# A raised scheduler priority for the ScalarE and VectorE steps of an RWKV-7 state passage

## The chip, the cores and the metric

The kernel runs on one core of a Trainium2 chip. The metric is the device time of one execution in microseconds (us). Engines are called PE (TensorE, matmuls), PEld (TensorE's weight loads), DVE (VectorE), ACT (ScalarE), POOL (GpSimd) and SP (SyncE, which here only issues transfers).

## The reference, cut to what matters

One layer of a hybrid trunk over 2048 tokens of width 1024. A token mixer takes one combined projection of the normed input and has three branches: chunked attention (4 heads), forgetting attention (4 heads) and RWKV-7 time mixing (8 heads). An output projection and a gated feed-forward part follow. The change touches the RWKV-7 branch alone, whose core is a recurrence over time:

```
def rwkv7_step(S, inp):
    r, w, k, v, kk, kka = inp
    sa = jnp.einsum('bhvk,bhk->bhv', S, -kk)
    S = S * w[:, :, None, :] + sa[..., None] * kka[:, :, None, :] + v[..., None] * k[:, :, None, :]
    y = jnp.einsum('bhvk,bhk->bhv', S, r)
    return S, y
...
    _, y = lax.scan(rwkv7_step, S0, xs)
```

## The kernel before

The program has three stages after one another: the input projection with the RWKV-7 branch (here called the mixer stage), then attention, then the output projection and the feed-forward part. Only the mixer stage is of interest.

The mixer stage handles 4 blocks of 512 tokens, and in each block 4 pairs of heads, so 16 rounds. A round of the recurrence is split into chunks of 64 tokens, 8 to a block. Three generators make the instructions of a round:

- `rwkv_front` projects the inputs (the matmuls of lines 281 to 283 in `project`), and forms decays, keys and the products of chunk with chunk (lines 411 to 507, most of them on DVE).
- `rwkv_inverse` inverts the triangular matrices of the chunks, by 31 pairs of small DVE operations that depend on one another (lines 533 and 536), and then by transfers and a few matmuls.
- `rwkv_back` carries the state through. It copies right-hand sides (`R`, line 608 by the helper of line 157), multiplies by the inverse (line 611), evicts `W` (line 157) and `UV` (line 616), multiplies again (line 626), forms `QA` (lines 634 and 637) and then goes through the 8 chunks: matmuls into `z` (lines 652 and 653), then the state `S` is rewritten by one ACT step (line 655) and one DVE step (line 656), and the next chunk's matmuls read it. The 16 rounds have 128 of these steps. After every 4 chunks the outputs are evicted into `Y` (line 658 on ACT, line 157 on DVE). All `z` of 4 chunks lie in one PSUM bank (`ZB = 1`).

The function `weave` writes these generators' instructions into one program: a back part and an inverse part of the round before go in between the projection matmuls of the present round. A back part that has issued a step yields a number of projection matmuls (`NEED`; 6 after each state step) before its next instructions are written.

This written order is not the order on the engines. A planner gives each instruction a number, in the order in which it is written. It then plays the program through by its own durations and, for each engine, takes the instruction with the lowest number among those whose inputs are there. What comes out is one fixed queue for each engine, which the chip then runs in that order, whatever the real durations are. Where an instruction's input is late on the chip, the whole queue of its engine waits.

Of the kernel before, what the change touches and what calls it, by code (L numbers as in the profile page):

```python
# [14 lines left out]
AF = mybir.ActivationFunctionType  # L15
ALU = mybir.AluOpType
# [4 lines left out]
P = 128  # L21
# [7 lines left out]
LEV = {'acc': G_, 'w': G_, 'kka': V, 'kf': V, 'rk': V, 'n': V, 'l': V, 'ql': V, 'ak': G_, 'gn': V, 'kr': V, 'uv': S_, 'r': V, 'w_': V, 'y': V, 'dt': V, 'bp': V, 'qa': V}  # L29
# [67 lines left out]
def trunk_kernel(ctx: ExitStack, tc: tile.TileContext, xT, w_in, pp, cst, cau, rel, relr, w2, a2, g2, w_out, w_up, w_down, out, dbg=None):  # L97
    nc = tc.nc
# [14 lines left out]
    def par(name, i=0):  # L113
        a = PP[name][0] + i
        return pps[:, a : a + 1]

    def cn(name):
        a, b = CC[name]
        return csts[:, a:b] if b <= 256 else cst1[:, a - 256 : b - 256]
# [36 lines left out]
    def copy(e, out, in_):  # L156
        e.copy(out, in_) if e is nc.scalar else e.tensor_copy(out=out, in_=in_)
# [79 lines left out]
    for r in range(NR):  # L237
        KR = c1.tile([P, 2, 8, 64], F32, name=f"KR{r}")
# [12 lines left out]
    for i in range(4):  # L251
        S = c1.tile([P, P], F32, name=f"S{i}")
# [259 lines left out]
    def rwkv_inverse(s):  # L512
# [53 lines left out]
        for c, e in ((0, nc.scalar), (1, LEV['dt'](nc))):  # L566
            rows = slice(c * 64, c * 64 + 32)
            copy(e, DT[rows, :, c * 64 + 32 : c * 64 + 64], ps[rows].rearrange("p w s i -> p (w s) i"))

    def rwkv_back(s):  # L570

        b, i, lg, KR, DT, LZ, v, bD, EC = (s[n] for n in ("b", "i", "lg", "KR", "DT", "LZ", "v", "bD", "EC"))
        S = Ss[i]
        Yt = t512("Y", "bp")
        Y = Yt.rearrange("p (a h d) -> p a h d", a=4, h=2)
        halves = (0, 2)
        UVs, Rs, Ws, QAs = {}, {}, {}, {}

        for p0 in halves:
            ps = psm["b"].tile([P, 2, 2, 2, 64], F32, name="rw", tag="ps")  # L580
            for a_ in range(2):
                pr = p0 + a_
                nc.tensor.transpose(ps[:, 0, a_].rearrange("p h d -> p (h d)"), v[:, pr * P : (pr + 1) * P], ident)
                nc.tensor.transpose(ps[:, 1, a_].rearrange("p h d -> p (h d)"), KR[:, 0, pr * 2 : pr * 2 + 2, :].rearrange("p c t -> p (c t)"), ident)
            UV = UVs[p0] = t512("UV", "bk").rearrange("p (a h c d) -> p a h c d", a=2, h=2, c=2)
            nc.scalar.copy(UV[64:128, :, :, 0, :], ps[0:64, 0])
            copy(LEV['uv'](nc), UV[0:64, :, :, 1, :], ps[64:128, 0])
            R = Rs[p0] = t512("R", "bk")
            nc.scalar.copy(R.rearrange("p (u s d) -> p u s d", u=4, s=2)[:, :, 0, :], ps[:, 1].rearrange("p a h d -> p (a h) d"))
        yield NEED[0]  # L590

        for p0 in halves:
            ps = psm["b"].tile([P, 4, 64], F32, name="rw", tag="ps")
            for u in range(4):
                a_, hp = divmod(u, 2)
                for c in range(2):
                    o = 64 - c * 64
                    mm(
                        ps[c * 64 : c * 64 + 64, u, :],
                        LZ[o : o + 64, p0 + a_, hp, c, 0, :],  # L600
                        UVs[p0][o : o + 64, a_, hp, c, :],
                        start=True,
                        stop=True,
                    )
            copy(LEV['r'](nc), Rs[p0].rearrange("p (u s d) -> p u s d", u=4, s=2)[:, :, 1, :], ps)
        yield NEED[1]
        yield NEED[3]
        for p0 in halves:
            ps = psm["b"].tile([P, 4, 2, 64], F32, name="rw", tag="ps")
            for u in range(4):  # L610
                mm(ps[:, u].rearrange("p s d -> p (s d)"), DT[:, p0 * 2 + u, :], Rs[p0][:, u * P : (u + 1) * P], start=True, stop=True)
            W = Ws[p0] = qd.tile([P, 4, 64], F32, name="W", tag="W")
            copy(LEV['w_'](nc), W, ps[:, :, 0, :])
            for c in range(2):
                rows = slice(c * 64, c * 64 + 64)
                nc.scalar.mul(UVs[p0][rows, :, :, c, :].rearrange("p a h d -> p (a h) d"), ps[rows, :, 1, :], -1.0)
        yield NEED[4]

        for p0 in halves:
            QA = QAs[p0] = t512("QA", "bk").rearrange("p (a c n) -> p a c n", a=2, c=2)  # L620
            pcs = [psm["b"].tile([P, 2, P], F32, name="rw", tag="ps") for c in range(2)]
            for u in range(4):
                a_, hp = divmod(u, 2)
                for c, ps in enumerate(pcs):
                    rows = slice(c * 64, c * 64 + 64)
                    mm(
                        ps[hp * 64 : hp * 64 + 64, a_, :],
                        Ws[p0][rows, u, :],
                        LZ[rows, p0 + a_, hp, c, 1:3, :],
                        start=True,  # L630
                        stop=True,
                    )
            for c, ps in enumerate(pcs):
                nc.vector.tensor_tensor(
                    QA[:, :, c, 0:64], KR[:, 1, p0 * 2 + c : p0 * 2 + 4 : 2, :], ps[:, :, 0:64], op=ALU.subtract
                )
                nc.vector.tensor_tensor(
                    QA[:, :, c, 64:128], cn("ident2").unsqueeze(1).to_broadcast([P, 2, 64]), ps[:, :, 64:128], op=ALU.subtract
                )
        yield NEED[5]  # L640

        for p0 in halves:
            if ZB == 2:
                zz = [ps_z.tile([P, 2, 2, 64], F32, name="z", tag="z") for c in range(2)]
            else:
                zt = ps_z.tile([P, 2, 2, 2, 64], F32, name="z", tag="z")
                zz = [zt[:, :, c] for c in range(2)]
            steps = [(a_, c) for a_ in range(2) for c in range(2)]
            for a_, c in steps:
                zs = zz[c][:, a_].rearrange("p h d -> p (h d)")  # L650
                for hp in range(2):
                    mm(zz[c][:, a_, hp, :], LZ[:, p0 + a_, hp, c, 1:3, :], UVs[p0][:, a_, hp, c, :], start=(hp == 0), stop=False)  # L652
                mm(zs, QAs[p0][:, a_, c, :], S, start=False, stop=True)
                ch = (p0 + a_) * 2 + c
                nc.scalar.activation(S[0:64, 0:64], zs[64:128, 0:64], AF.Identity, scale=EC[64:128, 0, ch : ch + 1])
                nc.vector.tensor_scalar(S[64:128, 64:128], zs[64:128, 64:128], EC[64:128, 1, ch : ch + 1], None, op0=ALU.mult)
                yield NEED[6]
            nc.scalar.copy(Y[0:64, p0 : p0 + 2], zz[0][0:64])
            copy(LEV['y'](nc), Y[64:128, p0 : p0 + 2], zz[1][0:64])

        Y8 = Y.rearrange("p a h d -> p (a h) d")
        st = sp.tile([P, 8], F32, name="st")
        nc.vector.tensor_reduce(st, Y8, axis=AX.X, op=ALU.add)
        nc.vector.tensor_scalar(st, st, 1.0 / 64, None, op0=ALU.mult)
        nc.vector.tensor_tensor(Y8, Y8, st.unsqueeze(2).to_broadcast([P, 8, 64]), op=ALU.subtract)
        ysq = t512("ysq", "bp")
        nc.scalar.activation(ysq, Yt, AF.Square)
        st2 = sp.tile([P, 8], F32, name="st2")
        nc.vector.tensor_reduce(st2, ysq.rearrange("p (g d) -> p g d", d=64), axis=AX.X, op=ALU.add)
        nc.scalar.activation(st2, st2, AF.Ln, scale=1.0 / 64, bias=eps[:, 1:2])  # L670
        nc.scalar.activation(st2, st2, AF.Exp, scale=-0.5)
        LEV['gn'](nc).tensor_tensor(Y8, Y8, st2.unsqueeze(2).to_broadcast([P, 8, 64]), op=ALU.mult)
        yield NEED[7]
        ps = psm["b"].tile([P, TB], F32, name="rw", tag="ps")
        for pr in range(4):
            nc.tensor.transpose(ps[:, pr * P : (pr + 1) * P], Y[:, pr].rearrange("p h d -> p (h d)"), ident)
        yl = t512("yl", "bp")
        nc.scalar.activation(yl, ps, AF.Identity, scale=par("lnx_g", i), bias=par("lnx_b", i))
        bv = t512("bv", "bp")
        nc.sync.dma_start(out=bv, in_=bD)  # L680
        nc.gpsimd.tensor_tensor(yl, yl, bv, op=ALU.add)
        gps = psm["b"].tile([P, TB], F32, name="rw", tag="ps")
        mm(gps, gg[:, i * P : (i + 1) * P], lg, start=True, stop=True)
        nc.vector.tensor_tensor(yl, yl, gps, op=ALU.mult)
        nc.gpsimd.dma_start(out=yD[512 + i * P : 512 + (i + 1) * P, b * TB : (b + 1) * TB], in_=yl)
# [505 lines left out]
    work, todo, Y = iter(()), None, None  # L1191
# [280 lines left out]
```

## Time and profile before

| | us |
|---|---|
| median of 3 runs (lowest, highest) | 3211.55 (3209.77, 3211.91) |
| the profiled execution, its own time | 3213.01 |
| its span, from the first to the last instruction | 3211.2 |
| the mixer stage, of the span | 0 to about 1175 |
| PE busy, of the span | 3017.4 (94%) |
| DVE busy, of the span | 2368.5 (74%) |
| ACT busy, of the span | 1394.9 (43%) |

The profile is one execution. In its rows a time of start is in us from the span's start. In a timeline a bracket behind a row gives the idle time of that engine just before it and the instruction whose end closed it. In the view of waits a row reads: who waited, for whom, us in total, how many times, and the longest.

### The profile page before, as it was taken

The page shows a single profiled execution, that of the slowest core. Times are in us where ns is not written, and L with a number is a line of the kernel's source. Part 1 is how long each engine was busy: PE and PEld are TensorE (multiplying, and loading weights), DVE is VectorE, ACT ScalarE, POOL GpSimd, SP SyncE. Part 2 cuts the span into 40 slices and gives each one's busy share as a digit, 9 for nine tenths or more (in the row PEclk, how much of TensorE's full clock was granted, in tenths as well). Part 3 has the DMA queues.
Part 4 walks back from the last instruction along what each step waited for, and adds up shares of the span by engine and source line. Part 5 has one row for each costly group of instructions (what it writes and reads, how often), then busy time and mean ns, then how long its engine had stood idle before and what let it go on. Part 6 is the DMA issues. An engine that isn't in the chain of part 4 may idle for free.

```text
span 3211.2 us, 49128 instructions
## 1 busy us (share of the span) xinstructions
PE 3017.4 (94%) x17820; PEld 2638.9 (82%) x17820; DVE 2368.5 (74%) x4590; ACT 1394.9 (43%) x2610; POOL 950.1 (30%) x928
## 2 busy tenths in 40 slices
PE   6988989998999979999989999999999998999999
PEld 4766767776767756677789899998899998999998
DVE  6667666756676646777553788889988889988886
ACT  5434444544444335578532343334333334333332
POOL 1010010001001021144242444444444444444443
PEclk8988999999999989999999999999999999999999
DMA  7756755656644576523234322222422222422221
GB/s 223 213 154 179 207 165 150 175 151 177 171 120 125 143 177 152 139 73 86 73 103 151 132 79 80 79 69 77 158 79 80 79 79 81 136 73 79 79 80 68
DMA packets 310818, 392.92 MB, mean 122 GB/s; under 512 B 137144, under 2 KB 228804, under 8 KB 299752
## 3 DMA queue, kind: packets, MB, share of 16 engines
q1 hardware_dynamic: 305936, 378.44, 40.0%
q0 software_dynamic: 2816, 8.39, 0.9%
q10 hardware_dynamic: 1824, 2.95, 0.4%
q8 instruction: 141, 2.31, 0.3%
q14 instruction: 101, 0.83, 0.1%
HBM read 304.65 MB, written 86.36 MB: 122 GB/s over the span
## 4 chain that ended last, share of the span: by engine, by line
PE 67%; DVE 17%; issue 5%; ACT 4%; DMA 4%; POOL 2%; SPq 1%; POOLq 0%; DVEq 0%; ACTq 0%
PE ps L1299 7%; PE ps L1298 7%; PE ps L1297 7%; PE ps L1345 4%; PE ps L1343 4%; PE ps L1344 4%; PE mm L282 2%; PE mm L281 2%; PE mm L283 2%; PE o L1069 2%; DVE tm L533 2%; DVE T L536 2%; PE z L652 2%; PE ps L1205 2%; PE ps L1206 2%
## 5 line engine op out<-in xcount | busy, mean ns | idle before, releaser
L1299 PE MATMUL ps<-B,wu 128*128 128x340 f32 (+1 forms) x1848 | 594.0, 321 | 19.6 <-DVE wu L161 19.4
L1297 PE MATMUL ps<-B,wu 128*128 128x340 f32 (+1 forms) x1848 | 589.7, 319 | 1.9 <-ACT wu L160 1.8
L1298 PE MATMUL ps<-B,wu 128*128 128x340 f32 (+1 forms) x1848 | 590.5, 320 | 0.0
L1299 PEld LDWEIGHTS ps<-B,wu 128*128 128x128 f32 x1848 | 348.7, 189 | 27.9 <-DVE wu L161 27.5
L1343 PE MATMUL ps<-hid,wd 128*128 128x340 f32 (+1 forms) x1056 | 341.9, 324 | 13.4 <-ACT wd L160 10.2
L1297 PEld LDWEIGHTS ps<-B,wu 128*128 128x128 f32 x1848 | 348.7, 189 | 2.6 <-ACT wu L160 2.1
L1298 PEld LDWEIGHTS ps<-B,wu 128*128 128x128 f32 x1848 | 347.8, 188 | 0.1
L1345 PE MATMUL ps<-hid,wd 128*128 128x340 f32 (+1 forms) x1056 | 338.8, 322 | 3.8 <-POOL wd L161 3.7
L1344 PE MATMUL ps<-hid,wd 128*128 128x340 f32 (+1 forms) x1056 | 340.1, 322 | 0.0
L281 PE MATMUL mm<-hT,w 128*128 128x512 f32 x704 | 314.5, 447 | 22.4 <-ACT w L160 16.0
L161 DVE TENSOR_TENSOR wu<-S,wu 128x512 fp32r<-128x512 f32 x264 | 258.0, 984 | 74.3 <-ACT wu L160 74.3
L282 PE MATMUL mm<-hT,w 128*128 128x512 f32 x704 | 291.2, 414 | 7.8 <-DVE hT L161 6.6
L283 PE MATMUL mm<-hT,w 128*128 128x512 f32 x704 | 291.3, 414 | 1.2 <-DVE w L161 1.1
L1346 DVE TENSOR_TENSOR acc<-acc,ps 128x340 f32<-128x340 f32 (+1 forms) x528 | 247.1, 502 | 48.1 <-PE ps L1345 47.8
L161 POOL TENSOR_TENSOR wd<-raw,wd 128x1024 fp32r<-128x1024 f32 x66 | 171.3, 2618 | 269.4 <-ACT wd L160 267.8
L160 ACT CAST wu<-S 128x512 fp32r<-128x512 f32 x264 | 162.9, 618 | 151.2 <-PE ps L1299 140.7
L1343 PEld LDWEIGHTS ps<-hid,wd 128*128 128x128 f32 x1056 | 201.6, 191 | 16.4 <-ACT wd L160 11.1
L1345 PEld LDWEIGHTS ps<-hid,wd 128*128 128x128 f32 x1056 | 201.6, 191 | 6.1 <-POOL wd L161 6.1
L161 DVE TENSOR_TENSOR wu<-raw,wu 128x512 fp32r<-128x512 f32 x198 | 201.1, 1017 | 5.6 <-ACT wu L160 5.6
L1344 PEld LDWEIGHTS ps<-hid,wd 128*128 128x128 f32 x1056 | 201.8, 191 | 0.0
L281 PEld LDWEIGHTS mm<-hT,w 128*128 128x128 f32 x704 | 138.8, 197 | 66.9 <-ACT w L160 17.0
L160 ACT CAST wu<-raw 128x512 fp32r<-128x512 f32 x198 | 120.7, 620 | 162.0 <-PE ps L1299 142.1
(337 smaller groups left out, 6814.2 us busy)
## 6 DMA issues: line engine op xcount, KB each, us to landing
w<-wD SPq DMA_DIRECT2D x72, 1024.0 KB, 6.6
raw<-in_w_up_dram SPq DMA_DIRECT2D x132, 512.0 KB, 3.6
raw<-in_w_down_dram SPq DMA_DIRECT2D x66, 512.0 KB, 3.6
wD<-w SPq DMA_DIRECT2D x24, 1024.0 KB, 5.5
wraw<-in_w_in_dram SPq DMA_DIRECT2D x24, 512.0 KB, 6.3
xt<-in_xT_dram SPq DMA_DIRECT2D x48, 256.0 KB, 4.2
K<-qkD SPq DMA_DIRECT2D x21, 512.0 KB, 8.3
Q<-qkD SPq DMA_DIRECT2D x84, 128.0 KB, 2.9
```

The costliest lines, as they stand in the source:

```text
L160: (hi_eng or nc.scalar).copy(hi, src) if (hi_eng or nc.scalar) is nc.scalar else hi_eng.tensor_copy(out=hi, in_=src)
L161: (lo_eng or nc.vector).tensor_tensor(lo, src, f(hi), op=ALU.subtract)
L281: mm(ps, hi[:, kt, 0:P], hT[kt][:, 0, :], start=(kt == 0), stop=False)
L282: mm(ps, hi[:, kt, 0:P], hT[kt][:, 1, :], start=False, stop=False)
L283: mm(ps, lo[:, kt, 0:P], hT[kt][:, 0, :], start=False, stop=(kt == KT - 1))
L1297: mm(ps, whl[:, 0, kt, :], Bs[p][:, kt, 0, 0:n], start=(kt == 0), stop=False)
L1298: mm(ps, whl[:, 0, kt, :], Bs[p][:, kt, 1, 0:n], start=False, stop=False)
L1299: mm(ps, whl[:, 1, kt, :], Bs[p][:, kt, 0, 0:n], start=False, stop=(kt == 3))
L1343: mm(ps, wd[:, 0, ch], hid[:, 0, cs], start=(u == 0), stop=False)
L1344: mm(ps, wd[:, 0, ch], hid[:, 1, cs], start=False, stop=False)
L1345: mm(ps, wd[:, 1, ch], hid[:, 0, cs], start=False, stop=(u == G - 1))
L1346: nc.vector.tensor_tensor(acc[ct][:, cs], acc[ct][:, cs], ps, op=ALU.add)
```

## The change

A context manager lowers the planner's number of every instruction written inside it by 200 and restores it on exit. It is put around the evictions and state steps of `rwkv_back`: `R` (one half of it), `W`, `UV`, `QA`, `S` on both engines, and `Y` on both engines. Matmuls, transfers and all other generators keep their numbers. No instruction is added, removed or altered; no tile is allocated inside the blocks.

```diff
+    def urgent():
+        return tc.high_priority(offset=200)
+
     def rwkv_back(s):
...
-            copy(LEV['r'](nc), Rs[p0].rearrange("p (u s d) -> p u s d", u=4, s=2)[:, :, 1, :], ps)
+            with urgent():
+                copy(LEV['r'](nc), Rs[p0].rearrange("p (u s d) -> p u s d", u=4, s=2)[:, :, 1, :], ps)
...
-            copy(LEV['w_'](nc), W, ps[:, :, 0, :])
-            for c in range(2):
-                rows = slice(c * 64, c * 64 + 64)
-                nc.scalar.mul(UVs[p0][rows, :, :, c, :].rearrange("p a h d -> p (a h) d"), ps[rows, :, 1, :], -1.0)
+            with urgent():
+                copy(LEV['w_'](nc), W, ps[:, :, 0, :])
+                for c in range(2):
+                    rows = slice(c * 64, c * 64 + 64)
+                    nc.scalar.mul(UVs[p0][rows, :, :, c, :].rearrange("p a h d -> p (a h) d"), ps[rows, :, 1, :], -1.0)
...
             for c, ps in enumerate(pcs):
-                nc.vector.tensor_tensor(
-                    QA[:, :, c, 0:64], KR[:, 1, p0 * 2 + c : p0 * 2 + 4 : 2, :], ps[:, :, 0:64], op=ALU.subtract
-                )
...
+                with urgent():
+                    nc.vector.tensor_tensor(
+                        QA[:, :, c, 0:64], KR[:, 1, p0 * 2 + c : p0 * 2 + 4 : 2, :], ps[:, :, 0:64], op=ALU.subtract
+                    )
...
                 ch = (p0 + a_) * 2 + c
-                nc.scalar.activation(S[0:64, 0:64], zs[64:128, 0:64], AF.Identity, scale=EC[64:128, 0, ch : ch + 1])
-                nc.vector.tensor_scalar(S[64:128, 64:128], zs[64:128, 64:128], EC[64:128, 1, ch : ch + 1], None, op0=ALU.mult)
+                with urgent():
+                    nc.scalar.activation(S[0:64, 0:64], zs[64:128, 0:64], AF.Identity, scale=EC[64:128, 0, ch : ch + 1])
+                    nc.vector.tensor_scalar(S[64:128, 64:128], zs[64:128, 64:128], EC[64:128, 1, ch : ch + 1], None, op0=ALU.mult)
                 yield NEED[6]
-            nc.scalar.copy(Y[0:64, p0 : p0 + 2], zz[0][0:64])
-            copy(LEV['y'](nc), Y[64:128, p0 : p0 + 2], zz[1][0:64])
+            with urgent():
+                nc.scalar.copy(Y[0:64, p0 : p0 + 2], zz[0][0:64])
+                copy(LEV['y'](nc), Y[64:128, p0 : p0 + 2], zz[1][0:64])
```

## Rows read from the trace of the kernel before

**Rows 1.** Mixer stage: us, busy (count) of PE PEld DVE ACT POOL, PEclk, DMA.

```profile
0.00:1175.00 1175.00, 1063.04 (x6266) 823.88 (x6266) 770.23 (x2173) 521.63 (x1073) 112.06 (x189) 0.94 0.60 167
```

**Rows 2.** The chain of work that ended last, from 1160 to 1212.

```profile
1173.90 0.86 PE rw L683 x2
...
1190.93 13.45 DMA TR<-exttD
```

**Rows 3.** Waits of PE in the mixer stage, 0 to 1175.

```profile
PE z L652 <- DVE S L656: 22.2, 18, 5.8
...
PE mm L282 <- DVE hT L161: 6.6, 3, 3.8
PE z L652 <- DVE Y L157: 6.0, 7, 2.0
...
PE z L652 <- ACT UV L616: 3.3, 3, 1.9
...
PE rw L683 <- DVE DT L157: 0.6, 1, 0.6
```

**Rows 4.** ACT's idle before line 655; line 656's durations, DVE's idle before it.

```profile
  PE z L653: 153.5, 97
...
L656 DVE TENSOR_SCALAR S<-z,EC x128: 290/291/294, 160.4 to 1165.4; 64x64 f32<-64x64 f32 x128
...
  ACT S L655: 58.3, 56
```

**Rows 5.** Timelines around the longest wait: PE and ACT, 455 to 478.

```profile
459.04 1.02 PE L427 MATMUL mm<-sq,cst 128*128 128x512 f32 x2
...
460.97 0.44 PE L653 MATMUL z<-S,QA 128*128 128x128 f32 x2
...
461.17 0.48 PE L281 MATMUL mm<-hT,w 128*128 128x512 f32 x1
...
467.28 0.39 PE L283 MATMUL mm<-hT,w 128*128 128x512 f32 x1
473.47 1.08 PE L652 MATMUL z<-UV,LZ 128*128 128x64 f32 x4 [5.80 <-DVE S L656]
...
463.23 0.31 ACT L655 ACTIVATE S<-z,EC 64x64 f32<-64x64 f32 x1
```

**Rows 6.** Timeline of DVE in that stretch: first and last before the step.

```profile
463.37 0.21 DVE L297 SCALAR_TENSOR_TENSOR r<-carry,pps,r 128x1 f32<-128x1 f32 x1
...
471.76 1.25 DVE L533 TENSOR_TENSOR tm<-T,NT 128x35 f32<-128x35 f32 x1
473.04 0.29 DVE L656 TENSOR_SCALAR S<-z,EC 64x64 f32<-64x64 f32 x1
```

**Rows 7.** Busy time and clock in and behind that wait (columns: Rows 1).

```profile
465.00:472.20 7.20, 2.67 (x12) 1.85 (x10) 7.20 (x12) 1.95 (x3) 5.01 (x5) 1.00 0.77 265
472.20:479.00 6.80, 5.53 (x20) 4.52 (x20) 4.22 (x15) 0.62 (x2) 0.75 (x1) 0.50 0.03 10
```

**Rows 8.** Timeline, 738 to 752: the two next waits, and what DVE ran.

```profile
743.36 0.66 PE L652 MATMUL z<-UV,LZ 128*128 128x64 f32 x4 [2.52 <-DVE S L656]
...
744.33 0.31 ACT L655 ACTIVATE S<-z,EC 64x64 f32<-64x64 f32 x1 [0.86 <-PE z L653]
...
749.76 0.29 DVE L656 TENSOR_SCALAR S<-z,EC 64x64 f32<-64x64 f32 x1
...
750.11 0.66 PE L652 MATMUL z<-UV,LZ 128*128 128x64 f32 x4 [3.01 <-DVE S L656]
```

**Rows 9.** Timeline, 408 to 412: a wait behind an operation that already runs.

```profile
409.11 1.56 DVE L438 TENSOR_SCALAR a<-a,pps,oka 128x512 f32<-128x512 f32 x1
...
411.05 0.66 PE L652 MATMUL z<-UV,LZ 128*128 128x64 f32 x4 [0.41 <-DVE S L656]
```

**Rows 10.** Timelines of PE: a wait with nothing in the way, one behind ACT.

```profile
309.03 1.12 PE L652 MATMUL z<-UV,LZ 128*128 128x64 f32 x4 [0.73 <-DVE S L656]
...
522.94 0.43 PE L652 MATMUL z<-UV,LZ 128*128 128x64 f32 x2 [1.90 <-ACT UV L616]
```

More of the change, by code (lines that the diff above doesn't have):

```diff
@@ L633, in rwkv_back @@
             for c, ps in enumerate(pcs):
-                nc.vector.tensor_tensor(
-                    QA[:, :, c, 0:64], KR[:, 1, p0 * 2 + c : p0 * 2 + 4 : 2, :], ps[:, :, 0:64], op=ALU.subtract
-                )
-                nc.vector.tensor_tensor(
-                    QA[:, :, c, 64:128], cn("ident2").unsqueeze(1).to_broadcast([P, 2, 64]), ps[:, :, 64:128], op=ALU.subtract
-                )
+                with urgent():
+                    nc.vector.tensor_tensor(
+                        QA[:, :, c, 0:64], KR[:, 1, p0 * 2 + c : p0 * 2 + 4 : 2, :], ps[:, :, 0:64], op=ALU.subtract
+                    )
+                    nc.vector.tensor_tensor(
+                        QA[:, :, c, 64:128], cn("ident2").unsqueeze(1).to_broadcast([P, 2, 64]), ps[:, :, 64:128], op=ALU.subtract
+                    )
         yield NEED[5]
```

## Prediction

> **What bounds the kernel now.** I read the busy time by stage first, since the change touches the mixer stage alone. There PE is busy 1063.0 us of 1175, DVE 770.2 and ACT 521.6 [rows 1]. PE is the fullest engine, and its granted clock has a mean of 0.94, so it is partly at the lower of its two levels. Next I asked what follows the stage. The chain of work that ended last runs from PE's last mixer matmuls at 1173.9 straight into the loads of the attention stage, whose last one ends at about 1204 [rows 2]. These loads start when the mixer is done, so whatever the mixer stage saves or loses should move all that follows by as much. The price of the change is thus PE's idle time in the mixer stage, before and after.
>
> That idle time is 1175 - 1063 = 112 us, and the view of PE's waits names who ended it. The largest single entry is the matmuls of the next chunk (line 652) that wait for the state's DVE step (line 656): 22.2 us in 18 waits, one of 5.8. Two other entries lie in the change's reach, `Y` with 6.0 and `UV` with 3.3 [rows 3]. With some small ones (`R`, `QA`) I sum the waits for steps that get the priority to 35 us in 33 waits. Between that and the rest there is a second sum that I need below: PE's waits for DVE work that gets no priority, from `hT` with 6.6 down to `DT` with 0.6 [rows 3], some 31 waits with 31.5 us together.
>
> **What the change does, part by part.** It adds and removes nothing. It moves ACT and DVE instructions forward in the fixed queues, where the planner saw them ready and other ready instructions with lower numbers went ahead. So a wait can shrink only if its state step stood behind instructions that *started* after the step's input was there. I went through the long waits by that test.
>
> *The long ones.* In the wait of 5.80 us, the matmuls of a chunk end at about 461.4, ACT's half is done at 463.54, and PE runs projection matmuls until 467.7 [rows 5]. DVE's half starts only at 473.04. DVE had been busy without a break, with 15 operations started in between, from the front's and the inverse's chains, the last one of 1.25 us [rows 6]. The planner knew of this delay: it put 27 projection matmuls behind the chunk, the first at 461.17 and the last at 467.28 [rows 5], instead of the 6 that `NEED` asks for. These DVE operations are numbered close to the step: the front's operations follow the matmul of line 427, which runs at 459.04, just ahead of the chunk [rows 5], so 200 is ample to pass them. With the priority DVE's half runs at about 464, PE still has its 27 matmuls, and the wait goes: 5.80 us. The two next ones are of the same make: waits of 2.52 and 3.01 us; in the second, ACT's half is done at 744.64 and DVE's starts at 749.76 [rows 8]. Both go, since the step would have had its turn before PE ran out. Sum: 5.80 + 2.52 + 3.01 = 11.3 us.
>
> [...]
>
> *The short ones.* Of the other 30 waits, several stand behind one operation that was already running when the step became ready; a priority doesn't stop it. An example is 0.41 us behind the 1.56 us of line 438 [rows 9]. Others are the bare way from PE over ACT (0.31) and DVE (0.29) back to PE, 0.73 us with nothing in the way [rows 4, 5, 10]. At four places something could go by the same test, 0.9, 1.1, 1.5 and 1.1 us, 4.6 together; the third is the wait of 1.90 us for `UV` [rows 10]. Against that, with another interleaving other steps will meet a running operation of 1.5 us. I take the short ones at zero, and keep 4.6 us for the range.
>
> *What it costs.* An instruction that moves forward moves those that it passes back by its own length: 0.29 us for a DVE state step [rows 4]. Who suffers is PE, where it already waits for such DVE work: 31 waits, so at most 31 x 0.29 = 9.0 us if each of them has a passed instruction ahead of it. Where PE doesn't wait for DVE now, its backlog of projection matmuls hides 0.29 us. The state steps, `W`, `R`, `QA` and `Y` are spread over the rounds, while the waits for `hT`, weights and the front's results sit at a few places, so I take a third: 3.0 us. The bounds are 0 and 9.0.
>
> ACT is busy 44% of the stage and waits for PE before 97 of its 128 state steps [rows 1, 4], so there is little for its priority to pass; at nothing. If this cover were gone, the price would be 0.31 us a step. No transfer is moved: none is issued within the blocks, and SP and POOL keep their own order but for what follows from earlier or later inputs.
>
> *The sum.* 11.3 + 3.4 - 3.0 = 11.7 us less. The profiled execution took 3213.0 us, 1.5 above the median; 3213.0 - 11.7 = 3201.3, and in terms of the median 3199.8.
>
> **The rivals.** *More of the same.* The priority also takes the 4.6 us of short waits and costs nothing: 11.3 + 3.4 + 4.6 = 19.3, so 3192. For it speaks that the steps would be prompt throughout; against it, that the running operations stay.
>
> *No change that can be measured* (within 0.2%, 6.4 us, which is about what a measurement of this kernel can tell from no change). The three long waits go, but others of their size arise. The stretch of the first has DVE full for 7.20 of 7.2 us and POOL busy for 5.0 [rows 7]; nothing in it becomes shorter, the same work only stands in another order, and what the front hands to PE comes later by all that passed it. The planner's queues for PE change too, and the projection matmuls that now cover other waits may stand elsewhere. About 3211.
>
> *Slower: the queue waits at its head.* The planner places a step where the step is ready by its own durations. On the chip PE may reach the chunk later; then DVE stands at the step with all behind it waiting, the inverse's chain and the front's. This happens now: before 56 of the 128 steps DVE is idle until ACT's half is done, 58.3 us together, about 1.04 us each [rows 4]. The other 72 steps are not waited for, partly because they stand late. If the priority makes 56 more of them wait as long, DVE's wait doubles, and I bound what reaches PE by doubling its waits for other DVE work: 31.5 us more. It decides where that outweighs 11.3 + 3.4 = 14.7, which is from 14.7 / 31.5 x 56 = 26 more waiting steps on. At 41 of them the loss is 23 us, the net 8.4 slower: about 3220. For it speaks that the queues are fixed and PE's clock falls at places that no plan can foresee; against it, that ACT, whose state step stands in front of DVE's, already waits for 97 of 128 chunks without PE being hurt. [...]
>
> *That the change does nothing* can hardly be: the 15 operations ahead of one ready step show that the order would differ, and the mixer's queues would differ from the first such step on.
>
> **How the numbers follow.** The forecast, 3192 to 3205 around 3199.8, gets 0.42, because the three long waits pass the test with large margins. More than that, under 3192, gets 0.06. No measurable change gets 0.28: the sum is less than twice the 6.4 us that can be told, and the reordering touches all 16 rounds. Slower gets 0.24. So faster by over 0.2% has 0.48, within it 0.28, slower 0.24. For 8 in 10 the range reaches from 3188 (the second case without its price and with some of the other low clock) to 3222 (the slower case just past its estimate), leaving out some 0.04 below and 0.13 above. The likeliest case's own range is 3192 to 3205.
>
> **What would show it.** Right: PE's waits of line 652 for line 656 fall from 22.2 to about 10 us with none over 1.6; no stretch at 0.50 clock behind a state wait in the second block; PE's last mixer matmul at about 1163 instead of 1174; attention and feed-forward as long as before. The cost shows in PE's waits for `hT`, `w`, `LZ` and `T`, from 31.5 to about 35 us. The slower rival shows as DVE's wait at line 656 for line 655, 58.3 us in 56 now, well over 85 us in over 82, with PE's waits for other DVE work above 46. The prediction is wrong if the long waits come back elsewhere, if the clock's low stretches move rather than go, or if the stages behind the mixer don't follow its end.

## The result: faster, by 0.3 to 0.6%

| | before | changed kernel |
|---|---|---|
| first comparison, median us (runs) | 3212.05 (6) | 3190.61 (6) |
| ratio, 95% interval | | 0.9937 [0.9920, 0.9954] |
| second comparison, median us (runs) | 3213.52 (33) | 3200.15 (12) |
| ratio, 95% interval | | 0.9967 [0.9952, 0.9982] |
| the profiled execution, its span | 3213.01, 3211.2 | 3200.97, 3199.2 |
| PE busy of the span | 3017.4 | 3007.5 |

The two intervals barely touch. Single executions of the changed kernel lie between 3186 and 3209 us, those of the kernel before between 3197 and 3229, so a comparison of this change wants some ten runs of each.

Behind line 568 the lines of the changed kernel have moved by 3 to 8: the chunk's matmuls are lines 658 and 659, the state steps 662 (ACT) and 663 (DVE), `UV` 621. In the kernels of the experiments they may lie another 1 to 4 lines further.

First the mixer stage of the two profiled executions up to its last matmul, before and after, in the columns of [rows 1], and the end of the changed kernel's stage on the chain that ended last (start, us, what):

```profile
0.00:1174.80 1174.80, 1062.84 (x6266) 823.80 (x6266) 770.23 (x2173) 521.43 (x1073) 111.86 (x189) 0.94 0.60 167
0.00:1166.10 1166.10, 1056.89 (x6266) 822.81 (x6266) 770.67 (x2173) 523.95 (x1073) 110.50 (x190) 0.94 0.60 169
```

```profile
1164.39 1.72 PE rw L691 x2
```

The stage ends at 1166.1 instead of 1174.8 [rows 2], 8.7 us earlier. The span is 12.0 us shorter; the other 3.3 lie in attention and feed-forward, whose instructions the change doesn't touch. There the time with a granted clock of 0.50 fell from 90.2 to 80.6 us. In a second trace of the changed kernel, with 94.5 us at 0.50, this part takes 2036.7 us, as long as before (2036.4). Within the mixer stage PE's idle time went from 112.0 to 109.2 us, by 2.8 alone. So the bulk of the 8.7 us is not idle time; it is PE's busy time, 1062.8 to 1056.9. The view of waits says what became of the idle time, against [rows 3 and 4]:

```profile
PE z L658 <- DVE S L663: 16.6, 20, 2.7
...
PE z L658 <- DVE Y L157: 10.6, 12, 2.2
...
PE z L658 <- ACT UV L621: 0.7, 1, 0.7
```

```profile
DVE S L663 <- ACT S L662: 56.1, 55, 4.6
```

The waits for the state fell from 22.2 to 16.6 us and those for `UV` from 3.3 to 0.7, while those for `Y` rose from 6.0 to 10.6. All waits for raised steps together went from 35.1 to 32.4. That is the first sign that the long waits didn't simply go. The timeline at the places of [rows 5 and 8] shows it, with two rows of DVE:

```profile
456.70 0.48 PE L281 MATMUL mm<-hT,w 128*128 128x512 f32 x1
...
457.95 0.40 PE L283 MATMUL mm<-hT,w 128*128 128x512 f32 x1
460.23 1.00 PE L658 MATMUL z<-UV,LZ 128*128 128x64 f32 x4 [1.89 <-DVE S L663]
...
469.86 0.29 DVE L663 TENSOR_SCALAR S<-z,EC 64x64 f32<-64x64 f32 x1
...
471.91 0.42 DVE L157 COPY Y<-z 64x256 f32<-64x256 f32 x1
...
472.47 0.63 PE L658 MATMUL z<-UV,LZ 128*128 128x64 f32 x4 [2.22 <-DVE Y L157]
...
737.30 1.12 PE L658 MATMUL z<-UV,LZ 128*128 128x64 f32 x4 [2.68 <-DVE S L663]
...
748.53 0.63 PE L658 MATMUL z<-UV,LZ 128*128 128x64 f32 x4 [0.88 <-DVE Y L157]
```

Where one wait of 5.80 us stood, there are two of 1.89 and 2.22, the second for the eviction `Y` that follows four chunks. Where 2.52 and 3.01 stood, there are 2.68 and 0.88. Of 11.3 us, 7.7 are still there. Two things differ from what was forecast. PE has only 6 projection matmuls behind the chunk ahead of the first of these waits, the first at 456.70 and the last at 457.95, where it had 27 [rows 5]. And a raised step isn't prompt: ACT's half of the fourth chunk's state step is done at 467.57, but DVE's half starts at 469.86, behind three operations that started in between, and the eviction `Y` comes after it, at 471.91.

### The profile page after: what moved, and what is told of

Same layout as the page of the kernel before. It is cut to its first block, busy times and chain, and to the rows that moved or that the text cites. A ratio compares the mean times of both kernels' runs of the same rounds, so it can differ in the third digit from the quotient of the medians.

```text
span 3199.2 us, 49138 instructions
## 1 busy us (share of the span) xinstructions
PE 3007.5 (94%) x17820; PEld 2634.3 (82%) x17820; DVE 2366.6 (74%) x4590; ACT 1398.1 (44%) x2610; POOL 955.5 (30%) x928
## 4 chain that ended last, share of the span: by engine, by line
PE 66%; DVE 17%; DMA 5%; issue 5%; ACT 4%; POOL 2%; SPq 1%; POOLq 0%; ACTq 0%; DVEq 0%
PE ps L1307 7%; PE ps L1306 7%; PE ps L1305 7%; PE ps L1351 4%; PE ps L1353 4%; PE ps L1352 4%; PE mm L283 2%; PE mm L281 2%; PE mm L282 2%; PE o L1077 2%; PE z L658 2%; DVE T L536 2%; DVE tm L533 2%; PE ps L1213 2%; DVE wu L161 2%
## 5 line engine op out<-in xcount | busy, mean ns | idle before, releaser
L1307 PE MATMUL ps<-B,wu 128*128 128x340 f32 (+1 forms) x1848 | 593.9, 321 | 19.7 <-DVE wu L161 19.6
L281 PE MATMUL mm<-hT,w 128*128 128x512 f32 x704 | 314.6, 447 | 20.8 <-ACT w L160 13.6
```

The costliest lines, as they stand in the source:

```text
L281: mm(ps, hi[:, kt, 0:P], hT[kt][:, 0, :], start=(kt == 0), stop=False)
L1307: mm(ps, whl[:, 1, kt, :], Bs[p][:, kt, 0, 0:n], start=False, stop=(kt == 3))
```

## The experiments

I put theory A (the gain is the three long waits for the state, which go), B (it is spread over all the passed steps) and C (any reordering of these fixed queues changes the time by about as much) against one another. The kernels differ only in which instructions get which number. The edits below are to the changed kernel, where it isn't said otherwise.

**The changed kernel once more**, unedited.

> The changed kernel once more, for its own scatter and a second trace. The executions so far lie at 3186 to 3201, the profiled one at the upper end with the same granted clock as before. If the 10 us between its executions are the clock's low stretches, a second trace that is faster shows less time at 0.50 clock, by about 20 us for 10 us of time. Expected ratio to before 0.992 to 0.9955 by all theories.

Ratio 0.9967, its 12 executions from 3188.5 to 3209.3 us. A busy row of the stretch of the long wait, and one of the changed kernel's first trace just behind it:

```profile
455.00:475.00 20.00, 15.78 (x91) 11.78 (x89) 18.91 (x48) 8.10 (x17) 9.74 (x9) 1.00 0.60 186
```

```profile
474.00:481.00 7.00, 7.00 (x36) 5.72 (x34) 3.04 (x11) 1.21 (x4) 0.74 (x5) 0.51 0.17 29
```

In the first trace the low clock still came behind that place (0.51), though the wait of 5.80 us was gone; in the second trace, whose waits there are 1.14 and 2.05 us at most, no clock record from 441 to 527 is under 1.00. PE's waits in the stage are much as in the first trace, 15.2 us for the state and 9.4 for `Y`. The same program, in the same order: the low stretches come and go between executions. By the clock records of the mixer stage this execution spent 114.7 us at half the clock, the first one 128.8, the one of the kernel before 129.7.

**The state steps alone.** Each block was given a letter (R; W with `UV`; Q; S; Y), so that the groups could be told apart:

```diff
-    def urgent():
-        return tc.high_priority(offset=200)
+    def urgent(what, s):
+        if what in 'S':
+            return tc.high_priority(offset=200)
+        return contextlib.nullcontext()
```

> Priority for the two S steps of each chunk alone; R, W, UV, QA and Y keep their numbers. Theory A (the gain is the three long waits for S that go): all of the gain, ratio about 0.994. Theory B (the gain is spread over all passed steps, evictions included): about half, 0.997. Theory C (any reordering gives some such change by chance): anything from 0.992 to 1.004.

Slower: 1.0044 [1.0022, 1.0065]. Theory A falls, and so does B, which had half of the gain here. The longest wait for the state is down as theory A wants it, yet `Y` takes its place, and other waits that were not there in [rows 3] arise:

```profile
PE z L661 <- DVE S L666: 15.5, 18, 2.4
PE z L661 <- DVE Y L158: 11.2, 11, 2.6
...
PE rw L634 <- DVE tm L534: 3.1, 2, 2.9
...
PE rw L618 <- DVE R L158: 2.5, 1, 2.5
```

PE's idle time in the stage is 117.5 us in this trace, 5.5 more than before.

**The evictions alone**, the complement.

```diff
+        if what in 'RWQY':
```

> Priority for R, W, UV, QA and Y; the S steps keep their numbers. Theory A: no change, 0.999 to 1.001, since the long waits stay. Theory B: the other half, about 0.997. Theory C: anything from 0.992 to 1.004.

Faster: 0.9970 [0.9953, 0.9988], as much as the whole change in the same comparison. And the three long waits are all there (5.5, 2.6 and 2.4 us; the first one's row below), which theory A had as the whole gain:

```profile
475.36 1.08 PE L661 MATMUL z<-UV,LZ 128*128 128x64 f32 x4 [5.52 <-DVE S L666]
```

```profile
0.00:1185.20 1185.20, 1082.96 (x6266) 839.32 (x6266) 773.62 (x2173) 522.37 (x1073) 113.68 (x190) 0.93 0.60 166
```

Idle time is 102.2 us, the least of all kernels. The execution that was profiled is the slowest of its 12 (3220.8 us against a median of 3204.5): it spent 174.1 us of the stage at half the clock. A single trace thus tells the total badly; the idle time may be steadier (the changed kernel's two traces have 109.2 and 109.8), but that is one pair.

**The whole change in two rounds only**, those with the three long waits.

```diff
+        if (s["b"], s["i"]) in ((1, 0), (2, 0)):
```

> The whole change, but only in the two rounds that hold the three long waits (first head pair of the second and third block). Theory A: nearly all of the gain, ratio about 0.994 to 0.996. Theory B: 2 of 16 rounds, so at most a fourth of it, 0.998 to 1.000. Theory C: a change of any size from this smaller reordering, 0.995 to 1.004.

1.0020 [1.0004, 1.0036], slower. PE's timeline in the two rounds:

```profile
461.43 0.66 PE L661 MATMUL z<-UV,LZ 128*128 128x64 f32 x4 [1.13 <-DVE S L666]
...
464.88 0.66 PE L661 MATMUL z<-UV,LZ 128*128 128x64 f32 x4 [1.13 <-DVE S L666]
...
473.47 0.63 PE L661 MATMUL z<-UV,LZ 128*128 128x64 f32 x4 [2.02 <-DVE Y L158]
...
741.59 1.12 PE L661 MATMUL z<-UV,LZ 128*128 128x64 f32 x4 [2.37 <-DVE S L666]
753.70 0.63 PE L661 MATMUL z<-UV,LZ 128*128 128x64 f32 x4 [3.22 <-DVE Y L158]
```

The wait of 5.80 us has become 1.13 + 1.13 + 2.02 and some small ones, those of 2.52 and 3.01 have become 2.37 and 3.22. What one step gained in the full DVE queue, later ones mostly gave back: 9.9 of the 11.3 us stand in these five waits. Theory A is out.

I formed theory D: the evictions bring the gain, and the state's priority costs. Now the evictions were split.

**R, W, `UV` and `QA`**, those ahead of the first state step:

```diff
+        if what in 'RWQ':
```

> Priority for R, W, UV and QA alone, the evictions ahead of the first state step; Y and S keep their numbers. Theory D (the evictions bring the gain and the S steps' priority costs, as PE's idle time in the mixer stage showed: 112.0 us before, 102.2 with evictions only, 117.5 with S only): if the part ahead of the state carries it, ratio about 0.997 to 0.998 and idle about 103 to 106; if Y carries it, 1.000 and 111. Theory C (chance of any reordering): no relation, 0.996 to 1.004.

**`Y` alone:**

```diff
+        if what in 'Y':
```

> Priority for the two Y evictions alone. Theory D: the rest of what e5 doesn't show, so that the idle times of this and of e5 fall by about 9.8 us together; PE's waits for Y fall from 6.0 to about 4.4 us as they did with all evictions, so alone hardly over 2 us: ratio 0.999 to 1.000. Theory C: 0.996 to 1.004.

1.0016 [0.9999, 1.0033] and 1.0014 [1.0000, 1.0028]: neither half of a gain of 0.3% is a gain. PE's idle time was 114.5 and 106.9 us. Theory D had the two idle times fall by about 9.8 us together; one rose by 2.5, the other fell by 5.1.

**Steps that no state step and no eviction waits for.** The kernel before, with 200 for its group norm:

```diff
+        with tc.high_priority(offset=200):
             nc.vector.tensor_reduce(st, Y8, axis=AX.X, op=ALU.add)
...
             LEV['gn'](nc).tensor_tensor(Y8, Y8, st2.unsqueeze(2).to_broadcast([P, 8, 64]), op=ALU.mult)
```

> The kernel before, with the same 200 for steps that no state and no eviction waits for: the group norm of the outputs behind the state passage (lines 663 to 672). Theory D: nothing for PE to gain, idle 110 to 114 us, ratio 0.999 to 1.001. Theory C: a change as large as those seen, over 0.3% either way, and idle off by 5 us or more.

0.9994 [0.9980, 1.0008], idle 112.8 us. Against theory C in its strong form: not every reordering changes the time.

**All evictions and the back part's first copies:**

```diff
+            with urgent("R"):
                 nc.scalar.copy(UV[64:128, :, :, 0, :], ps[0:64, 0])
                 copy(LEV['uv'](nc), UV[0:64, :, :, 1, :], ps[64:128, 0])
                 nc.scalar.copy(R.rearrange("p (u s d) -> p u s d", u=4, s=2)[:, :, 0, :], ps[:, 1].rearrange("p a h d -> p (a h) d"))
```

> Evictions only (R, W, UV, QA, Y), and also the three copies with which the back part begins (UV and the first half of R, lines 586 to 589), for which PE waits 6 to 7 us in every trace so far. Theory D: idle falls below 102, to about 98, ratio 0.995 to 0.997. Theory C: 0.996 to 1.004.

0.9971 [0.9953, 0.9989], idle 106.7 us instead of the expected 98. PE's waits for these copies did fall, from 6.7 to 4.4 us. No better than the evictions without them.

Two cells of the table of groups were missing, state with `Y` and state with the rest:

```diff
+        if what in 'SY':
```

> Priority for S and Y; R, W, UV and QA keep their numbers. Of the groups so far: S alone slower by 0.44% in the median, Y alone by 0.14%, and at the same granted clock (about 2.2 us for each 0.001 of clock, by 156 executions) S alone about 5 us slower, Y alone about 3 us faster. Theory E (the groups' effects add up): 2 us slower at the same clock, ratio 1.000 to 1.005. Theory F (S's priority costs by making Y late, PE's waits for Y went from 6.0 to 11.2 us, and Y's priority cures it): idle back from 117 to about 110, PE's waits for Y under 7 us, ratio 0.997 to 0.999.

```diff
+        if what in 'RWQS':
```

> Priority for S, R, W, UV and QA; Y keeps its number. Theory E: 3 us slower at the same clock, ratio 1.000 to 1.005. Theory F: Y stays late (10 us or more of waits), idle 113 to 118, ratio 1.001 to 1.005.

1.0022 [1.0007, 1.0038] and 1.0023 [1.0012, 1.0035], within what the sum of effects (theory E) allowed. Theory F, that the state's priority costs by making `Y` late, falls with the first: with its own priority `Y` is waited for as long as without it (12.0 us in that trace), and idle time stays at 117.8 us.

Two more changed the number itself:

```diff
-        return tc.high_priority(offset=200)
+        return tc.high_priority(offset=20)
```

> The whole change with 20 in place of 200. If what a step has to pass is numbered within some ten places, as I read it at the longest wait, the waits for S and Y come out as with 200 (15 to 17 and 9 to 11 us) and the ratio is 0.994 to 0.997. If most of what it passes is numbered farther away, the longest wait of 5.8 us stays and the ratio is 0.998 to 1.002.

0.9992 [0.9977, 1.0006]. The longest wait was split here too, into 2.0 and 4.0 us, but the gain is not there, and idle time is 118.6 us. PE's waits for the state and `Y` are 22.7 and 7.6 us, outside what I had expected if 20 were enough.

```diff
-        return tc.high_priority(offset=200)
+        return tc.high_priority(offset=-200)
```

> The whole change with the sign turned: the numbers of all these steps are raised by 200, so that they come after other ready work. If the order of these steps matters for PE as such, idle goes far over 112 us (130 to 160) and the ratio is 1.006 to 1.03. If PE's backlog of projection matmuls hides such delays, idle stays within 10 us of 112 and the ratio within 0.996 to 1.004.

1.0003 [0.9987, 1.0020], with idle time at 111.7 us. I had expected much idle time if the order of these steps mattered as such, and little change if PE's backlog of projection matmuls hides such delays; the second came. All of them got numbers 200 *higher*, and PE waits for them no more than before:

```profile
PE z L658 <- DVE S L663: 19.7, 18, 3.0
...
PE z L658 <- DVE Y L157: 5.0, 6, 2.5
```

So neither "first" nor "last" decides how long PE waits for the state: 16.6 us with the lower numbers, 22.2 with the written ones, 19.7 with the higher ones. The numbers do move the steps. By the prediction's own test, 33 of the 128 DVE state steps of the kernel before have operations ahead of them that started after ACT's half was done, 129 operations in all. With the change it is 21 steps and 40 operations, with the sign turned 37 and 177. The time from the end of ACT's half to the start of DVE's, summed over the 128 steps, is 73.7 us before, 39.5 with the change and 93.5 with the sign turned. Little of these differences reaches PE.

**All of it in one table.** Within each kernel's executions, time goes with the mean granted clock of the execution: over 239 executions in 16 groups the slope is -2.27 us for each 0.001 of clock (correlation -0.85). The last column moves each mean to the clock 0.967 with it; by the scatter that is left, such a mean is uncertain by about 1 us. Where an order itself brings on low stretches, the column takes out a part of its effect. The kernel before ran anew with each of three groups of kernels; its row gives the range. "R to QA" is R, W, `UV` and `QA`.

| what gets the priority | ratio | mean clock | idle us of PE in the stage (one trace) | mean us at clock 0.967 |
|---|---|---|---|---|
| nothing (before) | 1 | 0.9661 to 0.9671 | 112.0 | 3211.3 to 3212.6 |
| S | 1.0044 | 0.9628 | 117.5 | 3217.3 |
| R to QA | 1.0016 | 0.9645 | 114.5 | 3210.4 |
| Y | 1.0014 | 0.9641 | 106.9 | 3209.2 |
| S, Y | 1.0022 | 0.9638 | 117.8 | 3211.2 |
| S, R to QA | 1.0023 | 0.9632 | 112.2 | 3211.8 |
| R to QA, Y | 0.9970 | 0.9657 | 102.2 | 3203.2 |
| R to QA, Y and first copies | 0.9971 | 0.9675 | 106.7 | 3205.1 |
| S, R to QA, Y (the change) | 0.9937; 0.9967 | 0.9688; 0.9672 | 109.2; 109.8 | 3197.1; 3201.1 |
| the change with 20 | 0.9992 | 0.9678 | 118.6 | 3211.5 |
| the change with -200 | 1.0003 | 0.9657 | 111.7 | 3213.0 |
| the change in two rounds | 1.0020 | 0.9655 | 119.0 | 3215.7 |
| group norm only | 0.9994 | 0.9680 | 112.8 | 3211.5 |

Two things can be read from it. At the same clock the change gives 11 to 15 us, and the evictions without the state give 9 of them; R to `QA` or `Y` alone give 2 or 3. And the mean clock differs between the kernels by up to 0.006, which is 14 us, as much as the change is worth at one clock: the state alone, R to `QA`, `Y` and their pairs with the state have the lowest clocks and are slower in the median though most are no slower at the same clock.

The clock records allow one more split. In the trace of before, projection matmuls behind one another start 0.23 us apart at a granted clock of 1.00 (467.05 and 467.28) and 0.43 us apart at 0.50 (475.74 and 476.17), so about half of the busy time at 0.50 is the clock's. If half of the time that PE is busy at half the clock is taken out of its busy time in the stage, what is left is an estimate of its busy time at the full clock. It is 1009.1 us before and 1003.5 and 1004.4 in the changed kernel's two traces. The three other kernels that raise the state by 200 in all rounds have 1004.0 to 1006.4, all the rest 1007.4 to 1012.2. So, as far as one trace of each tells, the state's priority goes with a shorter busy time of the same matmuls, the evictions' with less idle time (102.2 and 106.7 us), and the change has some of both. Why the same matmuls are busy for less time is not shown.

## Why the prediction held, and where its reasons did not

**The size and the sign.** 11.7 us less were forecast; 21.4 were measured in the first comparison of medians and 13.4 in the second. In the profiled executions, against which the sum was made, it is 12.0. That the mixer's gain moves what follows held: 8.7 of the 12.0 us are there when the mixer ends. But that the number came out is luck. The forecast had 11.3 - 3.0 = 8.3 us from idle time and 3.4 from the clock. Of the 8.7 us measured, 2.8 are idle time, about 0.4 the clock (an estimate, half of the difference: PE was busy at half the clock for 107.5 us before and 106.7 after), and 5.5 are busy time at an equal clock, a term that the forecast doesn't have: it took PE's idle time for the whole price of the change. The second trace splits its 15.5 us at the stage's end into 2.2, 8.6 and 4.7. By two of its own signs of being wrong, too, the mechanism failed: long waits came back elsewhere, and low stretches of the clock moved rather than went.

**The three long waits, 11.3 us: the step that failed.** The test by which I counted them (did other operations start after the step was ready?) finds that a step was passed over. It doesn't say that PE waits less if it isn't. The forecast had the step run at about 464 with PE's 27 projection matmuls still behind the chunk. In the changed kernel the step runs early, but 6 stand there and PE waits 1.89 us: what covers a wait moved with the step. And in a stretch where DVE has no free time [rows 7], a later step, a state step or `Y`, is late in its place. 3.7 of the 11.3 us went. I had this as the rival "no change that can be measured": the long waits go and others of their size arise. That describes what the long waits did, and the two-rounds kernel shows that by themselves they are worth nothing or less.

**The clock behind the wait, 3.4 us.** No run shows this term, which was my estimate for a stretch at a granted clock of 0.50 that was to go with the first wait. It was too large by its own rows: PE was busy for 5.53 of the 6.8 us [rows 7], and half of that is 2.8. The stretch didn't go with the wait either: with the wait gone it was there in one trace (0.51 from 474 to 481) and not in another (1.00 from 455 to 475). Of all 14 traces, the six with a wait of 5.5 us or more at this place have a half-clock stretch that begins between 460 and 480 us, and so have seven of the eight in which the wait is shorter.

**The short waits, taken at zero.** Here is part of what the idle time lost: the waits for `UV` went from 3.3 to 0.7 us, in both traces of the changed kernel. By my own test 1.5 us of that stood in the trace of before [rows 10], and I left it out of the sum. The waits for `Y`, 4.6 us longer, were not foreseen at all.

**The cost, 3.0 us.** Not seen: PE's waits for DVE work without the priority sum to 28.9 us, against 31.5 before. It shows at the raised steps instead, in the waits for `Y`.

**The slower rival.** DVE idles before the state step for 56.1 us in 55 cases, against 58.3 in 56 [rows 4], so the queue doesn't wait at its head more than before. A step whose input is late does hold up what stands behind it: in 15 of the 56 cases before, DVE's operations next to the step on both sides are of the inverse's chain, so the one behind it needed nothing but what DVE had done before its idle time. In the longest of them line 533 is done at 955.92, DVE idles for 3.14 us, the step starts at 959.06 and line 536 at 959.38. But no early step brought the 23 us of loss that this rival had. The state's priority alone does cost, 0.44%, with this wait hardly longer (59.4 us in 58): its one trace has 5.5 us more idle time of PE, and its executions a lower mean clock, 0.9628.

**What stays open.** Why R to `QA` and `Y` have to be raised together is not settled. All three orders that raise both by 200 throughout are faster (0.9967, 0.9970, 0.9971), and none of the others is, by its interval. But the effects don't add up, 20 in place of 200 loses the gain, and the traces name no wait that accounts for it. The 5.9 us of PE's busy time in the profiled pair are hardly the clock's: the two stages have 129.7 and 128.8 us at half the clock. The second multiplication (line 626, behind the change 631) is the part whose busy time falls most, from 40.0 to 33.1 us in both traces of the change. With R to `QA` alone it is 35.5, and that kernel isn't faster. The clock's part (why one order has a mean of 0.963 and another 0.968) was measured, not explained. A weak form of theory C remains possible: that each of these orders has a time of its own within some 0.4%, and that the change found a good one.

## What to carry to other kernels

A wait behind a step that was passed over need not be worth its length: of the 11.3 us here, the longest of them in a stretch with DVE busy for 7.20 of 7.2 us, 3.7 went. In a full stretch, look for what will be late instead, and take the net. Test a priority by raising one group of steps at a time and by turning the sign: if "last" is as good as "first", the number is not what the time hangs on. Here that held for PE's waits, not for the time (0.9967 for "first", 1.0003 for "last"). Read PE's idle time and the granted clock as two terms, and compare orders over many executions.

## What the runs showed of the hardware

One program in one fixed order took from 3188.5 to 3209.3 us in 12 executions on one chip. The shortest had a mean granted clock of 0.971 and the longest 0.965; at 2.27 us for each 0.001 that is 13.6 of the 20.8 us between them. In the profiled executions before and with the change the clock records read 1.00 or 0.50 and nothing else, 28 of each before and 30 of each after. The stretches at half the clock, 108 to 174 us of the mixer stage in the 14 traces, stand at partly different places in two executions of the same program. I had taken such a stretch for a consequence of the wait in front of it.
